# One buffer for the high and the low part of a split weight tile

## The chip, the core and the metric

The kernel runs on one core of a Trainium2 chip. The metric is the device time of one execution in microseconds (us); the median of three runs of the kernel before is 1109.44 us (1108.57 to 1109.47). The engines are named as the profile names them: PE is TensorE (matmuls), PEld its weight loads, DVE VectorE, ACT ScalarE, POOL GpSimd, SP SyncE, which issues most DMAs.

## The reference

One layer of an encoder block on 256 positions of 2048 channels, float32. Only its matrix products matter here:

```python
proj = rmsnorm(h) @ w_in            # 2048 x 3616: z, xbc, dt, u
mix  = concat(ssd, pool) @ w_out    # 2048 x 2048
up   = rmsnorm(h) @ w_ffn_up        # 2048 x 11264: gate and value
ff   = (gelu(conv(gate)) * val) @ w_ffn_down   # 5632 x 2048
gate = sigmoid(rmsnorm(h) @ w_ple_gate)        # 2048 x 2048
h    = h + rmsnorm(gate * (p @ w_ple))
```

Between them stand a state-space mixer in chunks, pooling, depthwise convolutions and norms.

## The kernel before

Products are made in float32r, and for accuracy each operand is split: `hi` is the value cast to float32r (ACT, line 154), `lo` is the value minus `hi` (DVE, line 155). A product is then three: high by high, high by low, low by high. `split` (lines 142 to 156) makes both parts of one weight tile of 128 rows and up to 1056 columns from a raw tile that SP has loaded. The parts go to two rings of the pool `weights`, tags `whi` and `wlo`, each of five buffers of 1056 x 4 = 4224 bytes a partition. Raw tiles have a ring of three buffers of 8192 bytes (two weight tiles each), other data 13 "pages" of 8192 bytes.

The stages in order of time: `dtu` (the first projection, 16 weight tiles, lines 486 to 529), `xbc` (`feature_major`), `z` (`token_major`), the output projection `wo`, the up-projection, the down-projection `dn`, the gate `gt`. In `token_major` and `seven_products` the weight is the moving operand, 512 columns at a time. In `dtu` it is moving too, 352 columns; there the order `LOW_LAST` puts all products with the high part ahead of those with the low part.

In `feature_major` and in the up-projection (`feature_pairs`) the weight is the stationary operand. `feature_pairs` works through one weight tile (four k-slices, two blocks of 128 columns) in eight pairs of matmuls: the high part against 512 moving columns (activations high and low side by side), then the low part against 256 columns. The up-projection has 11 slabs, gate (`ug`, sums `ga`) and value (`uv`, sums `va`), each of eight weight tiles: 176 tiles. A tile's name counts slab, half, raw tile and part: `uv001_1` is slab 0, half 0, raw tile 1, second part.

The order on PE, DVE and ACT is set by the tile scheduler from priorities and estimated times, but inside the up-projection by `in_order`, which ties DVE, ACT and SP to the order of the code. A new tile of a ring waits until all readers of the buffer's last tile are done: its cast for those of the old `hi`, its subtraction for those of the old `lo`.

In the built program the ten buffers lie back to back from byte 42,848 of each partition, first the five of `whi`, then the five of `wlo`:

```
buffer        0      1      2      3      4
hi at      42848  47072  51296  55520  59744
lo at      63968  68192  72416  76640  80864
hi mod 256    96    224     96    224     96
lo mod 256   224     96    224     96    224

tile    uv000_0 uv000_1 uv001_0 uv001_1 uv010_0 uv010_1 uv011_0 uv011_1 ug100_0 ug100_1
buffer     2       1       0       4       3       2       1       0       4       3
```

Of the kernel before, what the change touches and what calls it, by code (L numbers as in the profile page):

```python
# [12 lines left out]
F32R = mybir.dt.float32r  # L13
# [4 lines left out]
P = 128  # L18
# [35 lines left out]
def build(nc, a, out):  # L54
# [6 lines left out]
    with tile.TileContext(nc) as tc, \  # L61
# [9 lines left out]
        def ins(r):  # L71
            return getattr(r, "ins", r)

        def page(name, dtype=F32):
            return gp.tile([P, 2048], dtype, tag="pg", bufs=13, name=name)
# [63 lines left out]

        spare, ready = {}, {}  # L140

        def split(name, src, nel, cuts=()):

            if name in ready:
                return ready.pop(name)
            if name in spare:
                hi, lo = spare.pop(name)
            else:
                hi = wp.tile([P, 1056], F32R, tag="whi", bufs=5, name=f"{name}h")
                lo = wp.tile([P, 1056], F32R, tag="wlo", bufs=5, name=f"{name}l")  # L150
            for c0, c1 in zip((0, *cuts), (*cuts, nel)):
                s = slice(c0, c1)
                if (name, c0) != ("dtu0", 0):
                    last["act"] = ins(nc.scalar.copy(hi[:, s], src[:, s]))
                last["dve"] = ins(nc.vector.tensor_sub(lo[:, s], src[:, s], hi[:, s].bitcast(F32)))
            return hi, lo
# [117 lines left out]
        def seven_products(name, stage, w, k0, c0, a_, acc, alt, start, stop):  # L274

            if (stage, c0, k0) in sums_:
                r = raw(f"{name}r")
                last["dma"] = load(r[:, 512:], w[c0 // 1024, k0 // 2][:, 512:], not name.startswith(IN_ORDER))  # L280
                t, held = sums_[stage, c0, k0]
                if not held:
                    t = lp.tile([P, 2048], F32, tag="own", bufs=1, name=f"{name}t") if name == "gt18" else page(f"{name}t")
                    last["dma"] = load(t, sums_[stage, c0, k0][0], not name.startswith((*IN_ORDER, "gt18")))
            else:
                r = t = raw(f"{name}r", w[c0 // 1024, k0 // 2])
                if stage in APART:
                    t = page(f"{name}t")
                    add_blocks(r, t)
            b11 = split(f"{name}a", r[:, 512:1024], 512)  # L290
            b2 = split(f"{name}b", r[:, 1024:], 1024)
            if r is t:
                add_blocks(r)
            t42 = split(f"{name}d", t[:, 1024:], 1024)
            t31 = split(f"{name}c", t[:, :1024], 1024)

            for x, (wh, wl), c, o, own in (
                    ("a11", b11, 0, alt[0], True), ("a12", b2, 0, acc[0][0], False), ("a22", t42, 0, acc[1][0], False),
                    ("s4", b2, 512, acc[0][1], False), ("s2", t42, 512, alt[3], True), ("s1", t31, 512, alt[1], True),
                    ("s3", t31, 0, alt[2], True)):  # L300
                xh, xl = a_[x]
                for q, (xx, ww) in enumerate(((xh, wh), (xh, wl), (xl, wh))):
                    mm(o, xx, ww[:, c:c + 512], own and start and q == 0, own and stop and q == 2)
# [173 lines left out]
                done = put(hn(k), x_part(k), vec(V_MIX + k))  # L477
            return done

        spare["dtu0"] = [wp.tile([P, 1056], F32R, tag=f"w{c}", bufs=5, name=f"dtu0{c[0]}") for c in ("hi", "lo")]  # L480
        turned = ins(nc.vector.tensor_copy(spare["dtu0"][0][:, :352], r0[:, :352]))
        with tc.issue_after(turned):
            front = x_panel(0, 1)
# [440 lines left out]
        h = [page(f"h{t}") for t in range(2)]  # L924
# [299 lines left out]
        for half in range(2):  # L1224
# [16 lines left out]
            for t in range(2):  # L1241
                for n, (o, c0) in enumerate(columns(acc[t])):
                    c1 = c0 + o.shape[-1]
                    c = slice(half * 1024 + c0, half * 1024 + c1)
# [102 lines left out]
```

## Time and profile before

| | us |
|---|---|
| median of three runs | 1109.44 |
| span of the profiled execution, first to last instruction | 1106.4 |
| PE busy | 1098.2 |
| DVE busy | 978.2 |
| ACT busy | 729.5 |
| POOL busy | 86.2 |

The page gives no other time of the profiled execution than its span. The stages, by busy time of each engine in a stretch (span, then busy us and number of instructions of PE, PEld, DVE, ACT, POOL; the clock granted to PE; share of the DMA engines; GB/s):

```profile
51.00:140.00 89.00, 88.81 (x713) 86.49 (x712) 82.95 (x153) 61.99 (x105) 3.15 (x5) 1.00 0.57 206
289.00:784.00 495.00, 495.00 (x2848) 434.58 (x2847) 433.20 (x614) 303.84 (x460) 28.19 (x54) 1.00 0.94 370
784.00:1004.00 220.00, 220.00 (x954) 178.59 (x953) 210.81 (x251) 172.49 (x220) 28.32 (x28) 1.00 0.94 373
```

The first is xbc, the second the up-projection, the third the down-projection. In each of them PE is busy nearly all the time at the full granted clock, and most of the kernel's time is in the second. Ends of matmuls are modelled, so the distance from one matmul's start to the next one's start says more of PE's pace than a busy time does; the timeline and the chain give starts to 0.01 us.

### The profile page before, as it was taken

To read this page: it belongs to the slowest core of one execution; us is meant where nothing else is said; L and a number is where in the kernel's file an instruction comes from. 1 tells how busy PE (TensorE), PEld (TensorE's weight loads), DVE (VectorE), ACT (ScalarE), POOL (GpSimd) and SP (SyncE) were. 2 spreads that over 40 slices of the span, in tenths; PEclk is the share of its full clock that TensorE was granted. 3 is DMA by queue.
4 is the path that set the end of the run, shared out by engine and by line. 5 is a ranking of instruction groups with operands and counts; after the bars stand their busy time and mean duration, and the time that the engine had idled before them with its cause. 6 is when DMAs were issued, how large, how long until landed. Compare 5 with 4: busy or idle time off the path is not lost.

```text
span 1106.4 us, 16113 instructions
## 1 busy us (share of the span) xinstructions
PE 1098.2 (99%) x5946; PEld 947.8 (86%) x5946; DVE 978.2 (88%) x1372; ACT 729.5 (66%) x1067; POOL 86.2 (8%) x145
## 2 busy tenths in 40 slices
PE   9999999999999999999999999999999999999997
PEld 9999988888888888888888888888888888888886
DVE  6589998898868998889889988888999999999996
ACT  6958763556775565565756646657688878777773
POOL 0200000100100000000000000000000000051001
PEclk9999999999999999999999999999999999999998
DMA  9985358556589999989999998999999999995872
GB/s 366 364 336 187 111 191 346 209 211 231 182 356 400 400 403 349 394 350 367 386 359 373 369 394 335 405 356 421 357 408 370 376 346 388 414 384 220 315 270 76
DMA packets 57247, 361.71 MB, mean 327 GB/s; under 512 B 6352, under 2 KB 7504, under 8 KB 21200
## 3 DMA queue, kind: packets, MB, share of 16 engines
q1 hardware_dynamic: 45648, 298.71, 69.4%
q0 software_dynamic: 11088, 61.35, 14.4%
q8 instruction: 47, 0.77, 0.3%
q10 hardware_dynamic: 432, 0.62, 0.2%
q14 instruction: 32, 0.26, 0.1%
HBM read 306.65 MB, written 54.00 MB: 326 GB/s over the span
## 4 chain that ended last, share of the span: by engine, by line
PE 97%; ACT 1%; DVE 1%; issue 0%; POOL 0%; POOLq 0%
PE ga L90 22%; PE va L90 22%; PE dna L90 11%; PE woa L90 6%; PE xbc L90 5%; PE gt L90 5%; PE dns L90 4%; PE dtu L90 4%; PE z L90 4%; PE dn0s L90 2%; PE dn1s L90 2%; PE ple L90 1%; PE gts L90 1%; PE yd L90 1%; PE wos L90 1%; PE pw L90 1%
## 5 line engine op out<-in xcount | busy, mean ns | idle before, releaser
L90 PE MATMUL ga<-wox,ug_0h 128*128 128x512 f32 x352 | 125.5, 395 | 0.0
L90 PE MATMUL ga<-wox,ug_1h 128*128 128x512 f32 x352 | 125.2, 394 | 0.0
L90 PE MATMUL va<-wox,uv_0h 128*128 128x512 f32 x352 | 124.8, 393 | 0.0
L90 PE MATMUL va<-wox,uv_1h 128*128 128x512 f32 x352 | 124.8, 393 | 0.0
L90 PE MATMUL ga<-wox,ug_1l 128*128 128x256 f32 x352 | 99.1, 282 | 0.0
L90 PE MATMUL va<-wox,uv_0l 128*128 128x256 f32 x352 | 99.1, 281 | 0.0
L90 PE MATMUL va<-wox,uv_1l 128*128 128x256 f32 x352 | 99.1, 281 | 0.0
L90 PE MATMUL ga<-wox,ug_0l 128*128 128x256 f32 x352 | 99.1, 281 | 0.0
L272 DVE TENSOR_TENSOR dnb<-dnb 128x512 f32<-128x512 f32 x128 | 88.3, 690 | 3.0
L90 PEld LDWEIGHTS va<-wox,uv_0h 128*128 128x128 f32 x352 | 66.1, 188 | 15.0
L90 PEld LDWEIGHTS ga<-wox,ug_1h 128*128 128x128 f32 x352 | 66.1, 188 | 15.0
L90 PEld LDWEIGHTS va<-wox,uv_1h 128*128 128x128 f32 x352 | 66.1, 188 | 15.0
L90 PEld LDWEIGHTS ga<-wox,ug_0h 128*128 128x128 f32 x352 | 66.1, 188 | 14.8
L90 PEld LDWEIGHTS ga<-wox,ug_0l 128*128 128x128 f32 x352 | 66.2, 188 | 0.1
L90 PEld LDWEIGHTS ga<-wox,ug_1l 128*128 128x128 f32 x352 | 66.2, 188 | 0.0
L90 PEld LDWEIGHTS va<-wox,uv_0l 128*128 128x128 f32 x352 | 66.2, 188 | 0.0
L90 PEld LDWEIGHTS va<-wox,uv_1l 128*128 128x128 f32 x352 | 66.2, 188 | 0.0
L247 POOL DMA_DIRECT2D dns<-dnb x30 | 16.1, 536 | 321.8 <-DVE dnb L272 281.0
L843 ACT CAST he<-he 128x512 fp32r<-128x512 f32 x13 | 8.1, 621 | 41.9 <-DVE he L842 41.9
L985 ACT CAST hs<-hid 128x384 fp32r<-128x384 f32 (+1 forms) x44 | 23.4, 536 | 13.6 <-PE dna L90 13.3
L1065 ACT ACTIVATE fc<-gr,vt 128x256 f32<-128x256 f32 x44 | 26.1, 593 | 6.2 <-DVE gr L1058 6.1
L1136 POOL DMA_DIRECT2D hd<-hsum x24 | 12.9, 539 | 193.4 <-PE dn0s L90 83.1
(2491 smaller groups left out, 3300.4 us busy)
## 6 DMA issues: line engine op xcount, KB each, us to landing
dnb<-w_down SPq DMA_DIRECT2D x32, 1024.0 KB, 10.3
dns<-dnb POOLq DMA_DIRECT2D x30, 1024.0 KB, 6.8
hd<-hsum POOLq DMA_DIRECT2D x24, 512.0 KB, 8.3
zr<-w_z SPq DMA_DIRECT2D x8, 1024.0 KB, 4.9
dtur<-w_dtu SPq DMA_DIRECT2D x14, 528.0 KB, 8.5
hsum<-he POOLq DMA_DIRECT2D x13, 512.0 KB, 7.6
wo0r<-w_out_ SPq DMA_DIRECT2D x6, 1024.0 KB, 7.0
gtb<-w_gate SPq DMA_DIRECT2D x6, 1024.0 KB, 10.0
```

What stands on the lines that cost most here:

```text
L90: last["pe"] = ins(nc.tensor.matmul(o, lhsT, rhs, start=start, stop=stop, skip_group_check=True))
L247: nc.gpsimd.dma_start(t, pg[0])
L272: nc.vector.tensor_add(s[:, i], v[:, i], a[:, b])
L843: nc.scalar.copy(o[:, :512], s[:, :512])
L985: nc.scalar.copy(t[:, :c1], hid_part(k)[:, :c1])
L1065: nc.scalar.activation(c[:, f], v[:, f], AF.Identity, bias=vec(V_FCB + 4 * s + 2 * i + f), scale=vec(w + NF))
L1136: nc.gpsimd.dma_start(o.bitcast(F32), kept[k])
```

## The change

`split` no longer takes `hi` and `lo` from two rings but both from one: a tile of 2112 columns, 8448 bytes, five buffers, of which the first half is `hi` and the second `lo`. The first weight tile, made ahead as a spare, does the same. Nothing else is edited.

```diff
+        def weight_pair(name):
+            w = wp.tile([P, 2112], F32R, tag="w", bufs=5, name=f"{name}w")
+            return w[:, :1056], w[:, 1056:]
+
         def split(name, src, nel, cuts=()):
...
             if name in spare:
                 hi, lo = spare.pop(name)
             else:
-                hi = wp.tile([P, 1056], F32R, tag="whi", bufs=5, name=f"{name}h")
-                lo = wp.tile([P, 1056], F32R, tag="wlo", bufs=5, name=f"{name}l")
+                hi, lo = weight_pair(name)
...
-        spare["dtu0"] = [wp.tile([P, 1056], F32R, tag=f"w{c}", bufs=5, name=f"dtu0{c[0]}") for c in ("hi", "lo")]
+        spare["dtu0"] = weight_pair("dtu0")
```

Line numbers after line 141 grow by four or three: the cast is line 157, the subtraction 158. The five buffers take up the same 42,240 bytes from 42,848 on, and every other tile of the program keeps its place:

```
buffer        0      1      2      3      4
hi at      42848  51296  59744  68192  76640
lo at      47072  55520  63968  72416  80864
hi mod 256    96     96     96     96     96
lo mod 256   224    224    224    224    224
```

A buffer is now free when the readers of both parts are done, and the cast, which writes it first, waits for that. On VectorE, in the up-projection, slab 1 (`uv_0`, `uv_1` are the two parts of a raw tile; `h`, `l` and `w` at the end stand for high, low and pair; in brackets the engines or DMA queues waited for), before:

```order
L155 TENSOR_TENSOR uv_0l<-uv10r_3579,uv_0h 128x1024 [waits DMAHW3_49,PE_49,Activation_49]
L155 TENSOR_TENSOR uv_1l<-uv10r_3579,uv_1h 128x1024 [waits PE_49,Activation_49]
L1068 TENSOR_TENSOR fc_3572<-fc_3572,ft_3573 128x2x255 [waits Activation_49]
L1069 TENSOR_TENSOR fc_3572<-fc_3572,gr_3571 128x2x255 [waits DVE_49,Activation_49]
L272 TENSOR_TENSOR dnb_12_3533<-dnb_12_3533 128x512 [waits DMAHW2_49]
L272 TENSOR_TENSOR dnb_12_3533<-dnb_12_3533 128x512 [waits DVE_49] x3
L155 TENSOR_TENSOR uv_0l<-uv10r_3637,uv_0h 128x1024 [waits DMAHW4_49,PE_49,Activation_49]
L155 TENSOR_TENSOR uv_1l<-uv10r_3637,uv_1h 128x1024 [waits PE_49,Activation_49]
```

and now:

```order
L158 TENSOR_TENSOR uv_0w<-uv10r_3455,uv_0w 128x1024 [waits DMAHW3_49,PE_49,Activation_49]
L158 TENSOR_TENSOR uv_1w<-uv10r_3455,uv_1w 128x1024 [waits Activation_49]
L1071 TENSOR_TENSOR fc_3448<-fc_3448,ft_3449 128x2x255 [waits Activation_49]
L1072 TENSOR_TENSOR fc_3448<-fc_3448,gr_3447 128x2x255 [waits DVE_49,Activation_49]
L275 TENSOR_TENSOR dnb_12_3410<-dnb_12_3410 128x512 [waits DMAHW2_49]
L275 TENSOR_TENSOR dnb_12_3410<-dnb_12_3410 128x512 [waits DVE_49] x3
L158 TENSOR_TENSOR uv_0w<-uv10r_3511,uv_0w 128x1024 [waits DMAHW4_49,Activation_49]
L158 TENSOR_TENSOR uv_1w<-uv10r_3511,uv_1w 128x1024 [waits Activation_49]
```

Three of four subtractions no longer wait for PE; the order is the same. Over the whole program VectorE has 356 separate wait instructions in place of 447, and PE's matmuls raise a semaphore 758 times in place of 923.

Where the scheduler sets the order, a few instructions change places. On VectorE at the start of xbc (`xb` are weight tiles of xbc, `dt`, `u`, `rxb` and `sp` are small work behind the first projection), before:

```order
L155 TENSOR_TENSOR xb_0l<-xb2r_651,xb_0h 128x1024
L564 SCALAR_TENSOR_TENSOR dt<-dtu_0_90,rx0r,small 128x32
L566 TENSOR_SCALAR u<-dtu_1_91,rx0r 128x352
L155 TENSOR_TENSOR xb_1l<-xb2r_651,xb_1h 128x1024
L564 SCALAR_TENSOR_TENSOR dt<-dtu_0_92,rx1r,small 128x32
L566 TENSOR_SCALAR u<-dtu_1_93,rx1r 128x352
L445 COPY rxb<-rxbp 128x256
L574 TENSOR_SCALAR sp_615<-dt 128x64
L155 TENSOR_TENSOR xb_0l<-xb2r_711,xb_0h 128x1024
```

and now:

```order
L158 TENSOR_TENSOR xb_0w<-xb2r_635,xb_0w 128x1024
L567 SCALAR_TENSOR_TENSOR dt<-dtu_0_90,rx0r,small 128x32
L569 TENSOR_SCALAR u<-dtu_1_91,rx0r 128x352
L567 SCALAR_TENSOR_TENSOR dt<-dtu_0_92,rx1r,small 128x32
L569 TENSOR_SCALAR u<-dtu_1_93,rx1r 128x352
L448 COPY rxb<-rxbp 128x256
L577 TENSOR_SCALAR sp_599<-dt 128x64
L158 TENSOR_TENSOR xb_1w<-xb2r_635,xb_1w 128x1024
```

The second tile's subtraction (`xb_1`) has moved behind four small operations. On ScalarE in front of z (`z_0`, `z_1` are the parts of z's first raw tile, `th`, `E` and `w` belong to the mixer), before:

```order
L154 CAST z_0h<-zr_1716 128x1024
L699 ACTIVATE th_1403<-cv_1382 128x1024
L633 COPY E_642<-seg_1531 128x512
L708 ACTIVATE w_1538<-cbm,dt 128x128 x6
L635 ACTIVATE E_642<-E_642 128x512
L708 ACTIVATE w_1538<-cbm,dt 128x128 x2
L154 CAST z_1h<-zr_1716 128x1024
```

and now:

```order
L702 ACTIVATE th_1371<-cv_1350 128x1024
L636 COPY E_626<-seg_1495 128x512
L711 ACTIVATE w_1502<-cbm,dt 128x128 x8
L157 CAST z_0w<-zr_1676 128x1024
L638 ACTIVATE E_626<-E_626 128x512
L157 CAST z_1w<-zr_1676 128x1024
```

The first cast of z has moved behind th, one copy of E and all of w. Elsewhere PE takes one or two of xbc's matmuls on the other side of a small one, and at the start of the down-projection two casts and three operations on `hid` change places with their neighbours.

## The prediction

> **What bounds the kernel now.** I read the profile page first (busy shares), then the list of waits of TensorE (PE), then the chain that ended last, and at last single matmuls in the timeline.
>
> ```profile
> PE 1098.2 (99%) x5946; PEld 947.8 (86%) x5946; DVE 978.2 (88%) x1372; ACT 729.5 (66%) x1067; POOL 86.2 (8%) x145
> PE gof L90 <- ACT godg L1209: 1.9, 1, 1.9
> PE dtu L109 <- POOL ident masks.py:199: 1.4, 1, 1.4
> PE seg L90 <- ACT E L633: 0.2, 1, 0.2
> ```
>
> The second to fourth line are the whole list of PE's waits: 3.5 us of 1106.4, one at the start, one at the end, and none of them for a weight split (lines 154 and 155). So PE is fed all the time, and the end is set by how fast it takes one matmul after the other. A change of buffers can move the time in two ways only: by a wait that reaches PE, or by the pace of the stream itself. I looked at the pace in the up-projection, 495 us long, where nothing but `feature_pairs` runs on PE. The chain of waits, in pieces of 128 matmuls (eight weight tiles of 8 high and 8 low matmuls):
>
> ```profile
> 359.53 22.33 PE va L90 x128
> 381.86 22.37 PE ga L90 x128
> 404.23 22.33 PE va L90 x128
> 426.55 22.33 PE ga L90 x128
> 448.88 22.33 PE va L90 x128
> 471.21 22.33 PE ga L90 x128
> 493.54 22.37 PE va L90 x128
> ```
>
> The pieces are alike but for every fifth, which is 0.04 us longer. A period of five fits the ring of five buffers, not the matrix (a period of four tiles) nor the ring of raw tiles (three). So I looked at the first matmul of each of eleven tiles that follow each other, in the timeline:
>
> ```profile
> 314.71 0.39 PE L90 MATMUL va<-wox,uv_0h 128*128 128x512 f32 x1
> 317.49 0.39 PE L90 MATMUL va<-wox,uv_1h 128*128 128x512 f32 x1
> 320.31 0.39 PE L90 MATMUL va<-wox,uv_0h 128*128 128x512 f32 x1
> 323.08 0.39 PE L90 MATMUL va<-wox,uv_1h 128*128 128x512 f32 x1
> 325.86 0.39 PE L90 MATMUL va<-wox,uv_0h 128*128 128x512 f32 x1
> 328.67 0.39 PE L90 MATMUL va<-wox,uv_1h 128*128 128x512 f32 x1
> 331.45 0.39 PE L90 MATMUL va<-wox,uv_0h 128*128 128x512 f32 x1
> 334.26 0.39 PE L90 MATMUL va<-wox,uv_1h 128*128 128x512 f32 x1
> 337.04 0.39 PE L90 MATMUL ga<-wox,ug_0h 128*128 128x512 f32 x1
> 339.82 0.39 PE L90 MATMUL ga<-wox,ug_1h 128*128 128x512 f32 x1
> 342.63 0.39 PE L90 MATMUL ga<-wox,ug_0h 128*128 128x512 f32 x1
> ```
>
> The differences are 2.78, 2.82, 2.77, 2.78, 2.81, 2.78, 2.81, 2.78, 2.78, 2.81 us. Beside the table of buffers in the section on the kernel (tiles uv000_0 to ug100_1) the rule is plain: the second, fifth, seventh and tenth tile lie in buffers 1 and 3, where the high part begins 224 bytes past a multiple of 256 and the low part 96; the others lie in buffers 0, 2 and 4, with 96 and 224. **Two buffers of five make long tiles**, and nothing waits in them.
>
> **The change, part by part.**
>
> *Where the parts lie.* A buffer of 8448 bytes is 33 times 256, so all five pairs begin at the same remainder: high 96, low 224, which is the kind of the short tiles (the old size, 4224, is 16.5 times 256, so that every second buffer was shifted by 128). A short tile followed by a short one takes 2.77 or 2.78, taken as 2.775 (third and eighth difference). Ten tiles took 342.63 - 314.71 = 27.92; ten short tiles would take 27.75; the 0.17 is shared by four long tiles: 0.0425 us each. The chain agrees: eight tiles in a row hold three long tiles, or four in every fifth piece, and that one more costs 22.37 - 22.33 = 0.04 (0.03 to 0.05 by rounding). The stage has 11 x 2 x 8 = 176 tiles, two in five long: 70.4. The gain is 70.4 x 0.0425 = **3.0 us** (2.1 to 3.5 with 0.03 to 0.05). [...]
>
> *The stages with the weight as moving operand* (`token_major`, `seven_products`). There I find no such period. Pieces of 24 matmuls, and two of 48 from xbc:
>
> ```profile
> 207.45 5.55 PE woa L90 x24
> 213.88 5.57 PE woa L90 x24
> 976.91 5.54 PE dna L90 x24
> 127.83 5.72 PE xbc L90 x48
> 134.42 5.69 PE xbc L90 x48
> ```
>
> The first three differ by at most 0.03 us, 1.25 ns a matmul. There are about 2,000 such matmuls; half of that difference up or down gives ±1.2 us as bounds, and I take 0, since the rows show no order by buffer. In xbc the weight is stationary, as in the up-projection, but two tiles (48 matmuls) differ by 0.03 us at most: 12 such pairs, ±0.2 us, taken as 0 too.
>
> *The wait for a free buffer.* ScalarE's cast of a new tile waited for the last reader of the old high part, VectorE's subtraction for that of the old low part. Now the cast waits for both, the subtraction only for the cast.
>
> ```profile
> ACT ug_0h L154 <- PE va L90: 17.2, 10, 1.8
> 351.26 1.05 ACT L154 CAST uv_0h<-uv10r 128x1024 fp32r<-128x1024 f32 x1 [2.46 <-DMA uv10r<-w_up]
> 359.37 0.39 PE L90 MATMUL va<-wox,uv_0h 128*128 128x512 f32 x1
> 30.18 1.12 PE L90 MATMUL dtu<-dtu8l,hnh 128*128 128x352 f32 x6
> 30.38 1.08 ACT L154 CAST dtu13h<-dtur 128x1056 fp32r<-128x1056 f32 x1
> 42.73 0.48 PE L90 MATMUL dtu<-dtu13h,hnh 128*128 128x352 f32 x2
> ```
>
> In the up-projection casts do wait for PE (first row), but the low part is read last only one matmul after the high part, at most the 22.33 / 64 = 0.35 us of a pair, and a cast runs about 7 us ahead of its use (351.26 + 1.05 against 359.37). In `token_major` and `seven_products` the third product reads the high part again, so the high part was the last already and nothing moves. The most is lost in the first projection, where `LOW_LAST` puts six low matmuls behind the high ones: the cast of dtu13 started as dtu8's low matmuls began and would now start about 1 us later, with 42.73 - 31.46 = 11 us of cover. Cost 0; without that cover 1 us for each of some three tiles.
>
> *Instructions that go.* 91 separate waits on VectorE (447 to 356 in the built program) and 165 of PE's semaphore signals (923 to 758).
>
> ```profile
> L155 DVEq EVENT_SEMAPHORE  x319: 21/21/2758, 4.9 to 1081.8; - x160
> ```
>
> At the median 21 ns the first is 91 x 0.021 = 1.9 us of VectorE's sequencer, spread over an engine that PE never waits for: 0. The signals ride on matmuls; the ten differences above contain tile ends with signals and show no extra: 0 (bound: 10 ns of rounding each, 1.6 us gained).
>
> *Order.* At the start of xbc the subtraction of xb20_1 goes behind four small operations on VectorE; in front of z the first cast goes behind the work on th and w on ScalarE.
>
> ```profile
> 51.78 1.22 DVE L155 TENSOR_TENSOR xb_1l<-xb2r,xb_1h 128x1024 fp32r<-128x1024 f32 x1
> 52.91 0.25 DVE L564 SCALAR_TENSOR_TENSOR dt<-dtu,rx1r,small 128x32 f32<-128x32 f32 x1
> 53.99 1.23 DVE L155 TENSOR_TENSOR xb_0l<-xb2r,xb_0h 128x1024 fp32r<-128x1024 f32 x1
> 55.17 0.28 PE L90 MATMUL xbc<-hnh,xb_1l 128*128 128x256 f32 x1
> 127.33 1.06 ACT L154 CAST z_0h<-zr 128x1024 fp32r<-128x1024 f32 x1 [1.27 <-issue]
> 135.48 1.22 DVE L155 TENSOR_TENSOR z_0l<-zr,z_0h 128x1024 fp32r<-128x1024 f32 x1
> ```
>
> The small operations take 53.99 - 52.91 = 1.08 us, so the subtraction would end near 53.0 + 1.1 = 54.1, and PE wants it at 55.17: 1 us of cover, cost 0; without it, what is late comes back once, at most about 1 us. z's cast may slip by some 4 us; VectorE reads it only at 135.48. Cost 0. The other shifts (one matmul past another, two casts at the start of the down-projection) stay within the same stretch of work.
>
> *Sum.* The profiled span is 1106.4 us; the median of the runs shown, 1109.44, lies 3.0 above it for what is outside of the span, which the change leaves alone. 1106.4 - 3.0 = 1103.4 for the span, + 3.0 = **1106.4 us**, 0.27% faster.
>
> **The rivals.**
>
> *The place of the buffer does not carry over: no change.* The long tiles may come from something else that goes with buffers 1 and 3 in the present layout. For it: five places, one layout, one execution, and a difference of 1.5%. Against it: ten tiles of ten follow the remainder, and all other tiles of the kernel keep their places. Gain 0: 1109.4 us. The Trainium skill, SBUF — State Buffer, section "Who interferes with whom", says that TensorE's reads wait for nobody, and by that this rival is the rule; no row here tells why the two buffers differ.
>
> *The distance between the two parts counts: slower.* Before, low lay 21,120 bytes behind high in every tile; now it is 4,224. Since it never varied, no row separates it from the remainder. If the new distance makes every pair as long as in buffers 1 and 3, the 105.6 short tiles lose 0.0425 us each: +4.5 us, 1113.9. It decides once the mean tile is above the present 27.92 / 10 = 2.792 us. Against it: the remainder alone explains all ten differences, with the distance held fixed.
>
> *The later release reaches PE.* Price 1 us for each tile in the first projection, once the cover of 11 us is gone: within 0.2%, 1110.4 at one tile. That the parts share no buffer after all is ruled out by the order rows, which name one tile for both.
>
> **How the numbers follow.** Forecast 0.72, the place does not carry over 0.18, distance 0.07, later release 0.03. A measurement of this kernel can tell about 0.2%, 2.2 us, from no change: faster is below 1107.2, slower above 1111.7. Of the forecast's 0.72 I put 0.06 above 1107.2 (a price of 0.03 a long tile, or 1.2 us lost in the stages with moving weights). Faster 0.66; same 0.06 + 0.18 + 0.03 = 0.27; slower 0.07. The forecast's own range is 1105.2 (1.2 us gained where the weight moves) to 1107.6; to hold eight in ten it must reach the rival of no change: 1105.2 to 1109.6.
>
> **What would show it.** Right: the chain's pieces of 128 matmuls in the up-projection all have one length, 8 x 2.775 = 22.20, with no longer fifth; pieces of 24 in the later stages stay at 5.54 to 5.57; PE's waits stay 3.5 us. If the pieces still read 22.33 and 22.37, the place did not carry over; if 22.5, the distance counts. A row of PE's waits that names line 157 or 158 would show a wait that I priced at nothing. The forecast is wrong as a whole if the up-projection is not shorter by 2 to 3.5 us.

## The result and the profile after

The changed kernel takes 1105.46 us (median of five executions, 1104.6 to 1106.84) against 1109.44 before: a ratio of 0.9968, 95% interval 0.9956 to 0.998. The profiled span went from 1106.4 to 1102.8 us.

The changed kernel's page, busy time of each engine:

```profile
PE 1094.5 (99%) x5946; PEld 946.5 (86%) x5946; DVE 977.1 (89%) x1372; ACT 729.0 (66%) x1067; POOL 86.5 (8%) x145
```

And its whole list of PE's waits (the tile that waited, what it waited for, then sum, count and longest, in us):

```profile
PE gof L90 <- ACT godg L1212: 1.9, 1, 1.9
PE dtu L109 <- POOL ident masks.py:199: 1.4, 1, 1.4
PE seg L90 <- ACT E L636: 0.2, 1, 0.2
```

PE still waits 3.5 us in all, at the same three places, and is busy 3.7 us less with the same 5946 matmuls. So no wait went or came: the stream of matmuls is quicker. The chain that ended last (start, length, what), with the pieces of 128 matmuls of the up-projection and pieces of the output and down-projection:

```profile
229.77 22.29 PE woa L90 x96
...
359.95 22.19 PE va L90 x128
382.14 22.19 PE ga L90 x128
404.33 22.19 PE va L90 x128
426.51 22.19 PE ga L90 x128
448.70 22.19 PE va L90 x128
470.89 22.19 PE ga L90 x128
493.07 22.19 PE va L90 x128
...
781.50 5.53 PE dna L90 x24
973.92 5.52 PE dna L90 x24
```

The reader should see that every piece is 22.19 now: the longer fifth piece is gone and the others have lost 0.14 us. On VectorE the waits that stand as separate instructions at the subtraction fell as the order rows said, from 319 to 230 profiled instructions, and the longest of them from 2.8 us to 0.1:

```profile
L158 DVEq EVENT_SEMAPHORE  x230: 21/21/107, 4.9 to 1078.3; - x115
```

Where the time went, by stages (from the start of a stage's first matmul to that of the next stage's first, read off the timeline; the up-projection from the tile uv000_0 on; the stretches left out, before, between and behind these stages, change by 0.1 us or less from before to after). The last five columns belong to experiments below; dn begins with the first matmul of the down-projection and ends, as gt begins, with the first that reads a tile `gt_0`; gt ends 23 to 24 us before the span does, where a tile `gt_0` is read again behind the tiles `gth` and `gtl`:

| us | before | after | place alone | share alone | both at 96 | both at 96, again | by stage |
|---|---|---|---|---|---|---|---|
| xbc | 87.93 | 88.26 | 88.01 | 88.18 | 88.55 | 88.54 | 87.06 |
| z | 55.73 | 55.62 | 55.63 | 55.73 | 55.01 | 55.05 | 55.01 |
| wo | 87.03 | 87.48 | 87.48 | 87.03 | 85.66 | 85.63 | 85.66 |
| up-projection | 469.05 | 465.92 | 465.92 | 469.05 | 465.92 | 474.88 | 470.40 |
| dn | 229.72 | 229.00 | 229.26 | 230.33 | 227.01 | 227.43 | 227.27 |
| gt | 69.13 | 68.77 | 69.49 | 69.14 | 68.16 | 68.16 | 68.18 |

Of the 3.6 us that the span lost, 3.13 are in the up-projection; the rest is the difference of small gains (dn 0.7, gt 0.4) and losses (wo 0.45, xbc 0.3).

Some kernels below were executed at one of two times, 4 to 10 us apart at the same granted clock, so their times are given in two groups and not as a median alone.

### The profile page after: what moved, and what is told of

Its sections match the earlier page's. It is cut to its first block, busy times and chain, and to the rows that moved or that the text cites. A ratio compares the mean times of both kernels' runs of the same rounds, so it can differ in the third digit from the quotient of the medians.

```text
span 1102.8 us, 16019 instructions
## 1 busy us (share of the span) xinstructions
PE 1094.5 (99%) x5946; PEld 946.5 (86%) x5946; DVE 977.1 (89%) x1372; ACT 729.0 (66%) x1067; POOL 86.5 (8%) x145
## 4 chain that ended last, share of the span: by engine, by line
PE 97%; ACT 1%; DVE 1%; issue 0%; POOL 0%; POOLq 0%
PE ga L90 22%; PE va L90 22%; PE dna L90 11%; PE woa L90 7%; PE xbc L90 5%; PE gt L90 5%; PE dns L90 4%; PE z L90 4%; PE dtu L90 4%; PE dn0s L90 2%; PE dn1s L90 2%; PE ple L90 1%; PE gts L90 1%; PE wos L90 1%; PE yd L90 1%; PE pw L90 1%
## 5 line engine op out<-in xcount | busy, mean ns | idle before, releaser
L90 PE MATMUL ga<-wox,ug_0w 128*128 128x512 f32 x704 | 130.8, 337 | 0.0
L90 PE MATMUL ga<-wox,ug_1w 128*128 128x512 f32 x704 | 130.2, 337 | 0.0
L90 PE MATMUL va<-wox,uv_1w 128*128 128x512 f32 x704 | 129.2, 336 | 0.0
L90 PE MATMUL va<-wox,uv_0w 128*128 128x512 f32 x704 | 129.2, 336 | 0.0
L90 PEld LDWEIGHTS ga<-wox,ug_0w 128*128 128x128 f32 x704 | 107.6, 188 | 14.6 <-ACT pl L919 0.2
L90 PEld LDWEIGHTS ga<-wox,ug_1w 128*128 128x128 f32 x704 | 107.5, 188 | 14.5 <-DVE wox L195 0.2
L90 PEld LDWEIGHTS va<-wox,uv_0w 128*128 128x128 f32 x704 | 107.5, 188 | 14.5
L90 PEld LDWEIGHTS va<-wox,uv_1w 128*128 128x128 f32 x704 | 107.5, 188 | 14.5
L90 PE MATMUL xbc<-hnh,xb_0w 128*128 128x256 f32 x192 | 37.9, 284 | 0.1
L90 PE MATMUL xbc<-hnh,xb_1w 128*128 128x256 f32 x192 | 37.1, 283 | 0.0
```

What stands on the lines that cost most here:

```text
L90: last["pe"] = ins(nc.tensor.matmul(o, lhsT, rhs, start=start, stop=stop, skip_group_check=True))
```

## The experiments

The theory after the result: the place of a part modulo 256 sets the pace of the matmuls that read it. The rivals: sharing as such (fewer waits and signals, later release), and the new distance of 4,224 bytes between the parts. In all of these kernels the order of instructions on ScalarE, VectorE, PE and SyncE is that of the kernel from which they are made. Tiles of the first projection need all 1056 columns and keep their place wherever the others are moved.

**Place alone.** The kernel before with its two rings; `SHIFTED` names the 189 tiles that land in buffers 1 and 3.

```diff
                 lo = wp.tile([P, 1056], F32R, tag="wlo", bufs=5, name=f"{name}l")
+                if name in SHIFTED and nel <= 1024:
+                    hi, lo = hi[:, 32:], lo[:, 32:]
```

> Two rings as before, the order of all instructions as before; only tiles that land in buffers 1 and 3 begin 128 bytes further in, so that every high part lies at 96 and every low part at 224 modulo 256, still 21,120 bytes apart. If the place decides (my theory), the chain's pieces of 128 matmuls in the up-projection read 22.19 us as after the change and the time is 3 to 4 us below before, 1105.5 to 1106.5. If the shared buffer itself (fewer waits and signals, later release) made the gain, the pieces stay at 22.33 with every fifth at 22.37 and the time at 1109.4. If the distance of 4,224 bytes made it, likewise 22.33, 22.37 and 1109.4.

Measured: 1105.24 us (seven executions, 1104.94 to 1106.04) against 1108.27 for the kernel before on the same chip, ratio 0.9971 (0.996 to 0.9982). Its chain:

```profile
359.78 22.19 PE va L93 x128
381.96 22.19 PE ga L93 x128
404.15 22.19 PE va L93 x128
```

The whole gain of the up-projection, 3.13 us, is there with two rings, all the waits of before and a distance of 21,120 bytes. The span is 1103.7 us, 0.9 above that of the changed kernel; 0.7 of this is in gt (69.49 against 68.77). There 48 matmuls take, first in the changed kernel and then in place alone:

```profile
1046.17 11.01 PE gt L90 x48
1046.56 11.14 PE gt L93 x48
```

The remainders of the weights are the same in both, so in gt something beside the remainder counts. It may be the distance between the parts, or a second pace as found further down; no run tells the two apart.

**Share alone.** The changed kernel, with the tiles of buffers 1 and 3 moved on so that the mix of before comes back.

```diff
             w = wp.tile([P, 2112], F32R, tag="w", bufs=5, name=f"{name}w")
+            if name in SHIFTED and not name.startswith("dtu"):
+                return w[:, 32:1056], w[:, 1088:]
             return w[:, :1056], w[:, 1056:]
```

> One shared buffer as in the change, the order of instructions as in the change; tiles that land in buffers 1 and 3 begin 128 bytes further in, which gives the mix of before: two tiles in five at 224 and 96, the rest at 96 and 224, 4,224 bytes apart. If the place decides: pieces of 22.33 and every fifth 22.37, and a time within 1 us of before, 1108.5 to 1109.4. If sharing or the distance made the gain: 22.19 and 1105.5.

Measured: 1109.1 us (eleven executions, 1107.9 to 1110.55), ratio to before 1.0006 (0.9997 to 1.0015). The longer fifth piece is back:

```profile
359.68 22.33 PE va L93 x128
382.01 22.37 PE ga L93 x128
404.38 22.33 PE va L93 x128
```

So sharing itself, its fewer waits and signals and the distance of 4,224 bytes make nothing that these runs can see; the interval leaves room for 1.7 us. The table says the same of two stages, whichever way the buffers are shared: the up-projection is 465.92 with the new places and 469.05 with the old, wo 87.48 and 87.03. For dn, gt and xbc it does not say it, since there the two experiments differ by up to 0.7 us from the kernel with the same places.

**Which part.** The changed kernel again, every tile (but those of the first projection) at a chosen place in its buffer, `H` and `L` in columns:

```diff
+            if name.startswith("dtu"):
+                return w[:, :1056], w[:, 1056:]
-            return w[:, :1056], w[:, 1056:]
+            return w[:, H:H + 1024], w[:, L:L + 1024]
```

H, L = 0, 1088 puts both at 96, 32, 1056 both at 224, and 32, 1088 the high part at 224 and the low at 96.

> Shared buffer; every high part at 96 and every low part at 96 modulo 256 (4,352 bytes apart). Which part's place decides? If the high part's: pieces of 22.19, time as after the change, 1105.5. If the low part's: all tiles long, pieces near 22.55 (8 x (22.19 / 8 + 0.0437)), time near 1105.5 + 176 x 0.044 = 1113.2. If each part costs half: near 22.37 and 1109.4. If neither place but the sharing made the gain: 22.19.

> Shared buffer; every high part at 224 and every low part at 224 modulo 256 (4,096 bytes apart). The mirror of the run with both at 96: 22.55 and 1113.2 if the high part's place decides, 22.19 and 1105.5 if the low part's, near 22.37 and 1109.4 if each costs half, 22.19 if place does not matter.

> Shared buffer; every high part at 224 and every low part at 96 modulo 256, the kind of the long tiles before, now in all five buffers. If the high part's place decides in the up-projection: from before's rows (22.37 - 22.33 = 0.0437 more exactly for one long tile) pieces of 22.19 + 8 x 0.044 = 22.54, time 8 us over the changed kernel's, 1113. If sharing matters and place does not: 22.19 and 1105.5.

Measured, one piece of the up-projection from the chain of each kernel, first of both at 96:

```profile
380.75 22.19 PE ga L90 x128
```

The same piece in the chain of both at 224:

```profile
384.10 22.47 PE ga L90 x128
```

And in that of high at 224 and low at 96:

```profile
382.85 22.52 PE ga L90 x128
```

In these executions, one profiled of each kernel, the piece is 22.19 with the high part at 96, wherever the low part lies, and with the high part at 224 it is 22.47 or 22.52 (most pieces of the last chain are 22.53): in the up-projection it is the high part's place that counts most, with 0.06 for the low part's. High at 224 and low at 96 is the kind of the long tiles of before. Its up-projection takes 473.09 us, and two parts in five of that with three of 465.92 make 468.8; before has 469.05, so the mix of the two kinds accounts for it to 0.3 us. Both at 224 takes 1115.01 us (1114.48 to 1115.09), high at 224 and low at 96 takes 1112.0 (1111.05 to 1114.57). Both at 96 was a surprise: seven executions at 1099.29 to 1101.37 and three at 1109.24 to 1109.46, ratio over all of them 0.995 (0.9926 to 0.9974). The 5 us below the changed kernel come from stages in which the weight is the moving operand:

```profile
229.66 21.76 PE woa L90 x96
...
780.11 5.48 PE dna L90 x24
970.77 5.47 PE dna L90 x24
```

With the low part at 96 too, 96 matmuls of wo take 21.76 in place of 22.29, 24 of the down-projection 5.47 in place of 5.52.

**Own place or place beside the other operand.** An unused tile of 128 bytes at the front of both at 96 moves everything, weights and activations, by 128.

```diff
+        nc.gpsimd.memset(cp.tile([P, 32], F32, name="shim"), 0.0)
         mhalf = cp.tile([P, 4], F32, name="mhalf")
```

> As the run with both parts at 96, but an unused tile of 128 bytes stands at the front, so that every tile of the program, weights and activations alike, lies 128 bytes further: both parts and the other operand at 224 modulo 256. If a part's own remainder decides, this is the run with both at 224 again: 22.47 and about 1115. If what counts is whether a part has the same remainder as the other operand of its matmul (all activations lay at 96 so far), it is the run with both at 96 again: 22.19 and about 1100.

Measured: five executions at 1099.73 to 1101.25, five at 1109.5 to 1110.91; the profiled one has

```profile
380.36 22.19 PE ga L90 x128
```

Both at 224 is 22.47 with the activations at 96 and, in this execution, 22.19 with the activations at 224. So the remainder is not good or bad in itself. The stages in which the weight moves say the same: z and wo take 55.01 and 85.66 us with both at 96 and again with all at 224, but 56.00 and 87.60 with both at 224. What counts is how the weight lies to something that moved along with it. The other operand of the matmul is the nearest candidate, but raw tiles, pages and all other data moved too, so that it is the other operand is argued and not shown.

**How fine.** Both at 160 (H, L = 16, 1040) and both at 32 (48, 1072), activations at 96.

> Both parts at 160 modulo 256, activations at 96. How fine is the rule? If only the upper half of 256 counts (bit 7), 160 is as 224: pieces of 22.47, about 1115. If the distance of 64 bytes matters too, something between or beyond: no number. If it is a matter of 64-byte steps from 96 (96 good, everything else bad), 22.47 or more.

> Both parts at 32 modulo 256, activations at 96. If only bit 7 counts, 32 is as 96: pieces of 22.19 and about 1100. If only 96, the remainder of the activations, is good: 22.47 and about 1115.

Measured, the piece in the chain of both at 160:

```profile
381.79 22.61 PE ga L90 x128
```

And in the chain of both at 32:

```profile
383.67 22.62 PE ga L90 x128
```

The kernels take 1111.02 us (1110.71 to 1112.33) and 1118.32 (1117.73 to 1118.58). So it is not only a matter of 128 bytes on or off; in these executions 64 bytes off in either direction is worse than 128 in the up-projection. In xbc it is the other way: there both at 160 takes 87.32 us from first matmul to first matmul and both at 32 takes 87.37, against 88.55 with both at 96.

**Where two times come from.** Both at 96 twice more and all at 224 once more, unedited, on another chip.

> The kernel with both parts at 96 once more: of its ten timed executions seven lay at 1099.3 to 1101.4 us and three at 1109.2 to 1109.5, and the profile was of the first kind. A profile of the second kind would show where 9 us come from. If the pace of PE's stream is what differs (the two reads of a matmul, at the same remainder, fall in step or out of it), the pieces of 128 matmuls are longer in the whole up-projection, 22.4 to 22.6 in place of 22.19, and pieces of 24 in the later stages too, with no more waits on PE. If a load or a split comes late, the pieces stay at 22.19 and PE's list of waits names it, 9 us in all. If this one is of the first kind: 22.19 and 1100 again.

> As the look before it: 22.19 and 1100 if it is of the first kind; of the second kind 1109.4, with pieces of 22.4 to 22.6 if the pace differs, or 22.19 and 9 us more of waits on PE if something comes late.

> The kernel with everything at 224 once more (five of its ten executions at 1109.5 to 1110.9, five at 1099.7 to 1101.3): 22.19 and 1100 if it is of the first kind; of the second kind 1109.5, with pieces of 22.4 to 22.6 if the pace differs, or 22.19 and 9 us more of waits on PE if something comes late.

All three were of the second kind, 1108.75, 1109.23 and 1110.83 us. Two pieces of the up-projection from the chain of the first of them, both at 96:

```profile
381.23 22.61 PE ga L90 x128
403.84 22.62 PE va L90 x128
```

Its whole list of PE's waits:

```profile
PE gof L90 <- ACT godg L1214: 1.9, 1, 1.9
PE dtu L109 <- POOL ident masks.py:199: 1.4, 1, 1.4
```

No wait is added. The same program with the same places streams the whole up-projection at 22.61 in one execution and at 22.19 in another: 474.88 - 465.92 = 9.0 us. The spans differ by 8.6; the other stages of the table agree with the first kind to 0.4 us, and the first projection, which it leaves out, is 0.9 us shorter here. Worked out from the starts in the timeline (1341 pairs of the stage), the next matmul starts on average 236.5 ns after a high one in this execution and 230.0 in the first kind, but 116.8 and 116.7 after a low one, so the slower pace lies in the step from high to low. 474.88 is also what the up-projection takes with both at 160 and with both at 32. So a place allows two paces, and something else chooses; the pace stays for the stage. It is not the chip alone: both kinds of time were met on one chip in both at 96, in all at 224 and in the last experiment.

**A place for each stage.**

```diff
+            if name.startswith("xb"):
+                return w[:, 16:1040], w[:, 1040:2064]
+            if name.startswith(("dtu", "ug", "uv")):
+                return w[:, :1056], w[:, 1056:]
-            return w[:, :1056], w[:, 1056:]
+            return w[:, :1024], w[:, 1088:]
```

> Shared buffer as in the change, order as in the change; the place is chosen by stage: in the up-projection high 96 and low 224 as in the change, in xbc both at 160, in all other stages both at 96. If places act stage by stage, the time adds up from the stages of earlier runs: up-projection from uv000_0 on 465.92 (22.19 a piece, and in every execution, since the second pace of 22.61 was seen only with both parts at the remainder of the activations), xbc 87.3 in place of 88.3, wo 85.7, down-projection 103.1 + 124 and gate 40.8 + 27.4 as with both at 96: some 1099 us, all executions within 1.5 us of each other. If the second pace belongs to the program and not to the place, some executions lie near 1108. If a stage's pace depends on what ran before it, the sum does not hold and the time lies between 1100 and 1105.

Measured: 1103.07 us, ratio 0.9938 (0.9921 to 0.9955); two executions at 1097.69 and 1099.01, four at 1103.03 to 1103.94. All six are below every execution of the changed kernel, and the ratio to before is below its 0.9968 (0.9956 to 0.998), so this beats both kernels. The stages in which the weight moves and xbc came out as the sum had them. The up-projection did not:

```profile
379.53 22.40 PE ga L90 x128
401.93 22.40 PE va L90 x128
```

It has the very places of the changed kernel and takes 22.40 a piece here, 470.40 - 465.92 = 4.5 us more. The guess that high 96 and low 224 has one pace only is wrong: it has 22.19 and 22.40. That the two quicker executions had 22.19 fits their times, but no profile shows it.

## Why the prediction was right

*The place of the parts.* Right in mechanism and size: 3.0 us predicted, 3.13 measured in the up-projection, 22.20 a piece against 22.19. Place alone gives it without the shared buffer, and share alone does not give it. Two things in the reasoning were too simple. The remainder counts by how it lies to something else, the other operand as far as argued, and not by itself (all at 224). And the pace that I read from one execution is one of those that a place allows; the changed kernel's five executions and the seven of place alone lie within 1104.6 and 1106.84, so nothing shows that they met the other, but the last experiment shows that it exists at these places. That is luck as far as anyone could know: at 22.40 a piece the up-projection takes 470.40 us against 469.05 before, and the change would have lost 1.4 us there in place of gaining 3.1.

*The stages with the weight as moving operand: 0, ±1.2 us.* The sum lay within the bounds (wo + 0.45, z - 0.11, dn - 0.72, gt - 0.36, together - 0.7), but not for the reason given. I took the spread of pieces of 24 for noise; the place counts there too, and both at 96 moves these four stages by 55.73 + 87.03 + 229.72 + 69.13 - (55.01 + 85.66 + 227.01 + 68.16) = 5.8 us against before. In wo the loss is that of the places, since place alone loses the same 0.45. For dn and gt the source of the gain is not shown: share alone, at the old places, has dn 0.6 longer than before, and place alone has gt 0.4 longer, not shorter. So that the sum came out near 0 is in part luck. xbc, where the weight is stationary, changed by + 0.33 and not within ±0.2; share alone has + 0.25 there at the old places, place alone + 0.08, so the place is not the main source as far as one execution of each tells.

*The wait for a free buffer, the instructions that go, the order: 0.* Right as far as these runs can tell, for the whole kernel: PE's waits are the same three, and share alone, which has all three edits at the old places, lies at a ratio of 1.0006 (0.9997 to 1.0015).

*The rivals.* That the place does not carry over, and that the distance makes it longer, both fell: a distance of 4,224 bytes goes with 22.33 (share alone) and with 22.19 (the change), 21,120 with both as well (before and place alone). That is the up-projection; in gt the distance is not excluded.

*The sum.* 1106.4 predicted, 1105.46 measured; the span 1103.4 predicted, 1102.8 measured. The 0.6 between are the small terms above and the tail.

What stays open: what chooses between the two paces of a place at the start of the up-projection. All profiles agree in that it holds through the stage and that no wait of PE in it goes with it. Moving the start of the stage by a few matmuls, to see whether its timing chooses, was not tried. Nor was moving the activations alone, which would show whether it is they that the weight's place counts beside.

## What to carry to other kernels

When an engine is busy all the time and nothing waits, compare the pace of equal pieces of its work: a difference that comes back with the period of a buffer ring is a matter of where the buffers lie, and the size of a buffer can be the cure. Try a tile's place against that of the operand it is read with, stage by stage, and take several executions before believing a gain of half a per cent from it. An edit that looks like one of synchronisation may act by moving addresses only; a kernel that keeps the addresses and one that keeps the synchronisation tell the two apart.

## What the runs showed of the hardware

In this kernel the start-to-start time of float32r matmuls depends on where the weight lies within 256 bytes, beside the rest of the data: the activations, raw tiles and pages lay at one remainder, and moving everything together by 128 bytes changed nothing in z, wo or the quicker pace of the up-projection. In the up-projection (512 and 256 moving columns in turn, 64 pairs a piece) the pieces were 22.19 (high part at the activations' remainder), 22.47 and 22.52 (128 bytes off), 22.61 and 22.62 (64 bytes off); with the weight moving, 96 matmuls of wo took 21.76 us with both parts at the activations' remainder and 21.97 to 22.40 at all other places.

An equal remainder can also run at 22.61, so one piece's time does not tell the place: the same program at the same places runs a stage of 470 us at one of two paces, 22.19 or 22.61. With high at 96 and low at 224 two kernels ran it at 22.19 and one at 22.40, in one profiled execution of each. The granted clock lay between 0.997 and 0.999 in all of these executions.

The Trainium skill, SBUF — State Buffer, section "Who interferes with whom", gives TensorE two independent read ports, one for the moving operand and one for the weights, which wait for nobody. These runs show a dependence that this does not account for: with the weight's parts at 224 a piece takes 22.47 when the activations and all other data lie at 96, and 22.19 or 22.61 when they lie at 224 too. They do not show at which part of the chip it arises, so they do not settle whether the two ports wait.
